# Third chunk's output projection in front of the last heads, last gate loaded ahead, last squares summed by TensorE

## The chip, the cores and the metric

The kernel runs on one core of a Trainium2 chip. The metric is the time of one execution on the device in microseconds (us), of which the median over several runs is taken. One core has a matrix engine (TensorE, PE in the profile), a vector engine (VectorE, DVE), an activation engine (ScalarE, ACT), GpSimd (POOL) and SyncE (SP), which in this kernel only issues DMAs; ScalarE issues some too.

## The reference

A decoder trunk of two layers over 2048 positions of width 1024, all in float32. Layer 0 is a gated short convolution; the change does not touch it. Layer 1 is stick-breaking attention with 8 heads of 64 and a gate, an output projection and a last RMSNorm. Cut to that part:

```python
q, g = split(rmsnorm(x, norm_b) @ w_in_b)
z    = (q @ k.T) * 64 ** -0.5
l1m  = where(mask, log_sigmoid(-z), 0)            # strictly causal
o    = exp(where(mask, z + reverse_cumsum(l1m), -inf)) @ v
x    = x + (o * silu(g)) @ w_out_b                # 512 -> 1024
out  = x * rsqrt(mean(x * x, channels) + 1e-6) * norm_f
```

## The kernel before

Activations are held transposed, channels on the 128 partitions, in four chunks of 512 positions (chunk 3 has the longest attention). A float32 product is made of three matmuls: both factors are split into a high and a low part (`split`, L174 to L176: a cast on ScalarE, a subtraction on VectorE or GpSimd), and high times high, high times low and low times high are added in PSUM (`mm3`, L203 to L214; all large projections therefore share line L209).

Attention of one head and chunk (`attention`, L479) goes over chunks of keys. For each, four score tiles `z` (two matmuls each), two sigmoids on ScalarE into `R` and `w`, a running product along the keys on VectorE (`tensor_tensor_scan`, L514), a product (L518), then transposes on TensorE (`wt`, L526), a split of these (L175, L176) and matmuls into `av` (L535, L536). After the last key chunk the two halves of `av` are added into `ot` (L543, L544). GpSimd masks the diagonal and copies the carry (L509 to L513).

After attention of a chunk come these steps:

- `gated(c, k)` (L556) for each pair of heads `k`: the gate `sga` is loaded (L561), the attention output `ogr` too (L566), GpSimd multiplies (L567), and the result is split into `og`. For the last pair of chunk 3, `ot` is still on the core and VectorE multiplies (L563).
- `out_b(c, obs)` (L580): for each of 8 output tiles the weights are loaded, 12 matmuls go into `pob`, the residual `x1o` is loaded and added (L590), the sum is stored to `y_d`, ScalarE squares it and GpSimd adds the square to `acc` (L172).
- `out_stat(c)` (L597): `rstd` sums the squares over channels by four small products with `ones` (L127; the profile counts eight instructions), and takes the inverse root by small VectorE operations (L129 to L141).
- `out_norm(c)` (L601): `bcast` spreads the four columns of `rstd` over a tile (`dg`, L157, two matmuls `prb`, L158); then for 8 tiles a load `x2r` from `y_d` (L607), a scaling on ScalarE (L608), a product on GpSimd (L609) and a store (L610).
- For chunk 3, `out_b_last` (L620) instead: first the products over the first three pairs of heads (9 matmuls a tile into `pob`, added at L630), then the loads of the fourth part of the weights (`whl_obl`, L634); it yields -1.0 there. The rest runs when the last head is done: the gate and split of the last pair, three matmuls a tile into `pol`, an add (L642), a square, sums on VectorE and GpSimd (L649 to L653), `rstd`, and scaling and storing.

The code is written as generators that yield an estimated cost, and `merge` interleaves them: it always advances the stream with the least share of its total done, where the share may be raised to a power (`S7` = 2 for the last heads, which lets them run ahead: the other stream is at half of its total when the heads are at 0.7). The order on each engine is then made by the framework's scheduler from that order and from simulated readiness. Matmuls of the fill are tied to an earlier `av` matmul, the ninth last (`anchors`, `SLACK` = 8), so that they don't run too far ahead. `chain` puts generators in a row, `take` takes a cost's worth, `until` stops at a yielded value, `zipped` alternates. A product of 24 matmuls is one `LIN`; `TO` is 4 of them, one `out_b`.

Two merges matter here (L743 to L751): the `fill` with the first six heads of chunk 3, and the `tail` with the last two. Buffers in rotation: `lin` two PSUM banks, `st` one, `ld` five tiles, weights (`whl`) four, `t` four.

Of the kernel before, what the change touches and what calls it, by code (L numbers as in the profile page):

```python
# [8 lines left out]
F32 = mybir.dt.float32  # L9
# [5 lines left out]
P = 128  # L15
# [30 lines left out]
def kernel(  # L46
# [66 lines left out]
    def st(nm):  # L113
        return psum.tile([P, CH], F32, name=nm, tag="st", bufs=1)
# [2 lines left out]

        return sb.tile([P, 2, CH], F32R, name=f"{nm}_{k}", tag="act", bufs=NA)

    def rstd(acc, nm, y=None):  # L120


        acc = acc if isinstance(acc, (list, tuple)) else [acc]
        ps = st(f"pst_{nm}")
        for j in range(4):
            for i, a in enumerate(acc):
                nc.tensor.matmul(ps[:, j:j + 1], a[:, j * P:(j + 1) * P], ones[:, 0:1], start=i == 0, stop=i == len(acc) - 1)  # L127
        v = sb.tile([P, 4], F32, name=f"v_{nm}", tag="sv")
        nc.vector.tensor_scalar(out=v, in0=ps[:, 0:4], scalar1=1.0 / D, scalar2=EPS, op0=ALU.mult, op1=ALU.add)  # L129

# [30 lines left out]
    def rstd_bcast(acc, nm, both=False):  # L161
        return bcast(rstd(acc, nm), nm, both)
# [390 lines left out]

    og_t = {}

    def gated(c, k, r=None):  # L556

        og = act_tile(f"og_{c}", k)
        og_t.setdefault(c, []).append(og)
        sg = ld512(f"sga_{c}_{k}")  # L560
        nc.sync.dma_start(out=sg, in_=sg_d[c][k])  # L561
        if r is not None:
            nc.vector.tensor_mul(r, r, sg)  # L563
        else:
            r = ld512(f"ogr_{c}_{k}")
            nc.sync.dma_start(out=r, in_=og_d[c][k])  # L566
            nc.gpsimd.tensor_mul(r, r, sg)  # L567
        split(og[:, 0, :], og[:, 1, :], r)
# [51 lines left out]
    def out_b_last(c):  # L620
# [11 lines left out]
        wl = [w_tile(f"obl{i}", 4) for i in range(2)]  # L632
        for ob in range(KD):
            nc.sync.dma_start(out=wl[ob // 4][:, :, ob % 4, :].bitcast(F32), in_=split_d["ob", ob][:, :, 3, :])  # L634
        yield -1.0
        anchors.clear()
        gated(c, 3, last_ot[0])
        acc = [sb.tile([P, CH], F32, name=f"acc_x2{c}_{i}", tag="acc", bufs=2) for i in range(2)]
        for ob in range(KD):
            ps = lin(f"pol_{ob}")  # L640
            yield from mm3(ps, wl[ob // 4][:, :, ob % 4:ob % 4 + 1, :], og[3:4], kt=1)
            nc.vector.tensor_add(x2[ob], x2[ob], ps)  # L642
            if ob < 2:
                nc.scalar.activation(acc[ob], x2[ob], AF.Square)
            else:
                sq = t512(f"sq_x2{c}{ob}")
                nc.scalar.activation(sq, x2[ob], AF.Square)
                if ob in (2, 4):
                    nc.gpsimd.tensor_add(acc[0], acc[0], sq)  # L649
                else:  # L650
                    nc.vector.tensor_add(acc[1], acc[1], sq)
                if ob == 6:
                    nc.vector.tensor_add(acc[1], acc[1], acc[0])  # L653
        pb = rstd_bcast(acc[1], f"x2{c}", both=True)
        pbs = t512(f"pbs_{c}")
        nc.scalar.copy(pbs, pb)
        for k in range(KD):
# [60 lines left out]
    def heads(lo, hi, c):  # L718
        for hb in range(lo, hi):
# [5 lines left out]
            else:  # L725
# [53 lines left out]
```

## Time and profile before

| | us |
|---|---|
| median of three runs | 1880.44 (1878.28 to 1884.79) |
| the profiled execution | 1879.31 |
| its span, first to last instruction | 1877.6 |
| TensorE busy | 1771.9 (94%) |
| VectorE busy | 1261.9 (67%) |
| ScalarE busy | 772.7 (41%) |
| GpSimd busy | 450.4 (24%) |
| mean granted TensorE clock | 0.979 |

Durations and moments come from the profiled execution; its time is 1.7 us above its span. Busy time of TensorE counts overlapping matmuls once; the mean length of one matmul is longer than the distance between two starts. A line number is one of the kernel before; where a line is a helper's, the names of the tiles tell who called it.

### The profile page before, as it was taken

Reading aid. Unit: us, or ns where it says so; the run is one execution under the profiler, and the core shown is the slowest. Engines: PE = TensorE matmul, PEld = TensorE weight load, DVE = VectorE, ACT = ScalarE, POOL = GpSimd, SP = SyncE. Lnnn points to the kernel's source line nnn. Section 1 sums busy time; section 2 is a strip of 40 time slices with the busy share of each in tenths; the row PEclk is TensorE's granted clock in tenths of the full one; section 3 lists DMA queues with packets and bytes.
Section 4 is the critical chain, followed back from the end, with each engine's and each line's share of the span. In section 5 each row is a group of like instructions: output and inputs, shape, how many; then the busy total and the mean of one; then the engine's idle time right before and its main releaser. Section 6 shows DMA issues by size and latency. Waiting matters only on the chain.

```text
span 1877.6 us, 24951 instructions
## 1 busy us (share of the span) xinstructions
PE 1771.9 (94%) x8312; PEld 1447.6 (77%) x8312; DVE 1261.9 (67%) x1927; ACT 772.7 (41%) x1497; POOL 450.4 (24%) x822
## 2 busy tenths in 40 slices
PE   7999999999999999999999999999988998988783
PEld 5888888888778878887888888888766886866562
DVE  7876534554243364478785478787858889889984
ACT  6423212231232143345443244454535556556642
POOL 5100000101111032132221122232223214547543
PEclk9999999999999999999999999999999999999896
DMA  9999865697978798867677766566586667778763
GB/s 292 309 324 332 307 195 165 209 328 280 336 250 281 227 330 257 290 207 250 216 253 244 248 195 204 183 215 198 180 300 196 223 194 265 260 238 278 225 196 130
DMA packets 238480, 460.44 MB, mean 245 GB/s; under 512 B 18448, under 2 KB 133136, under 8 KB 213776
## 3 DMA queue, kind: packets, MB, share of 16 engines
q1 hardware_dynamic: 178272, 400.09, 63.0%
q10 hardware_dynamic: 59920, 58.74, 10.9%
q8 instruction: 66, 1.08, 0.2%
q14 instruction: 62, 0.51, 0.1%
q0 software_dynamic: 160, 0.02, 0.1%
HBM read 322.73 MB, written 136.05 MB: 244 GB/s over the span
## 4 chain that ended last, share of the span: by engine, by line
PE 74%; DVE 10%; DMA 7%; issue 4%; ACT 2%; POOL 2%; SPq 0%; ACTq 0%; POOLq 0%; DVEq 0%
PE pX L209 9%; PE pB L209 9%; PE po L209 9%; PE pG L209 9%; PE pC L209 8%; PE wt L526 4%; PE pv L209 4%; PE pk L209 3%; PE pq L209 3%; DVE R L514 3%; PE pg L209 3%; PE av L536 3%; PE av L535 2%; PE z L500 2%; PE z L501 2%
## 5 line engine op out<-in xcount | busy, mean ns | idle before, releaser
L514 DVE TENSOR_TENSOR_SCAN R<-R,R,ones 128x512 f32<-128x512 f32 x192 | 255.0, 1330 | 25.2 <-ACT R L503 24.7
L503 ACT ACTIVATE R<-z 128x512 f32<-128x512 f32 (+1 forms) x320 | 174.0, 544 | 185.0 <-PE z L501 72.7
L176 DVE TENSOR_TENSOR wtl<-wt,wth 128x512 fp32r<-128x512 f32 (+1 forms) x320 | 186.2, 601 | 79.9 <-ACT wth L175 76.8
L175 ACT CAST wth<-wt 128x512 fp32r<-128x512 f32 (+1 forms) x320 | 159.6, 528 | 184.7 <-PE wt L526 150.3
L518 DVE TENSOR_TENSOR w<-w,R 128x512 f32<-128x512 f32 (+1 forms) x320 | 207.7, 658 | 19.6 <-POOL R L511 2.1
L209 PE MATMUL pC<-h,whl_C 128*128 128x512 f32 x768 | 189.8, 396 | 11.0 <-ACT whl_C L175 8.0
L513 POOL COPY R<-R 128x1 f32<-128x1 f32 x192 | 117.4, 613 | 340.9 <-DVE R L514 308.6
L209 PE MATMUL po<-y,whl_o 128*128 128x512 f32 x768 | 189.2, 393 | 2.4 <-DVE x L394 2.0
L209 PE MATMUL pX<-h,whl_X 128*128 128x512 f32 x768 | 186.3, 392 | 1.3 <-DVE cv L354 1.3
L209 PE MATMUL pB<-h,whl_B 128*128 128x512 f32 x768 | 185.9, 392 | 0.0
L209 PE MATMUL pG<-h,whl_G 128*128 128x512 f32 x768 | 185.7, 392 | 0.0
L526 PE MATMUL wt<-ident,w 128*128 128x128 f32 x1088 | 176.8, 278 | 7.5 <-DVE w L518 4.5
L209 PEld LDWEIGHTS pC<-h,whl_C 128*128 128x128 f32 x768 | 143.5, 189 | 44.1 <-ACT whl_C L175 8.0
L505 ACT ACTIVATE w<-z 128x512 f32<-128x512 f32 (+1 forms) x320 | 172.1, 543 | 2.5 <-PE wt L526 2.4
L209 PEld LDWEIGHTS pX<-h,whl_X 128*128 128x128 f32 x768 | 143.5, 188 | 31.5 <-DVE cv L354 1.5
L209 PEld LDWEIGHTS po<-y,whl_o 128*128 128x128 f32 x768 | 142.7, 188 | 32.1 <-DVE x L394 2.2
L209 PEld LDWEIGHTS pB<-h,whl_B 128*128 128x128 f32 x768 | 143.5, 188 | 29.7
L209 PEld LDWEIGHTS pG<-h,whl_G 128*128 128x128 f32 x768 | 143.6, 188 | 29.5
L526 PEld LDWEIGHTS wt<-ident,w 128*128 128x128 f32 x1088 | 137.4, 143 | 36.0 <-DVE w L518 6.9
L536 PE MATMUL av<-wtl,vv 128*128 128x512 f32 (+1 forms) x320 | 127.3, 401 | 27.0 <-DVE wtl L176 26.5
L514 DVE TENSOR_TENSOR_SCAN R<-R,ones 128x512 f32<-128x512 f32 (+3 forms) x128 | 116.4, 915 | 37.0 <-POOL R L509 32.8
L500 PE MATMUL z<-kt,q 128*128 128x512 f32 (+1 forms) x320 | 129.3, 406 | 5.7 <-ACT w L505 2.8
(172 smaller groups left out, 2685.1 us busy)
## 6 DMA issues: line engine op xcount, KB each, us to landing
whl_o<-sw_o SPq DMA_DIRECT2D x24, 1024.0 KB, 5.3
kt<-k_d ACTq DMA_DIRECT2D x80, 256.0 KB, 4.0
vv<-v_d ACTq DMA_DIRECT2D x80, 256.0 KB, 3.7
whl_C<-sw_C SPq DMA_DIRECT2D x16, 1024.0 KB, 5.9
whl_X<-sw_X SPq DMA_DIRECT2D x16, 1024.0 KB, 5.3
whl_B<-sw_B SPq DMA_DIRECT2D x16, 1024.0 KB, 5.8
whl_G<-sw_G SPq DMA_DIRECT2D x16, 1024.0 KB, 5.3
whl_k<-sw_kv SPq DMA_DIRECT2D x16, 1024.0 KB, 7.0
```

The lines of the kernel that those rows point to most:

```text
L175: nc.scalar.copy(hi, src)
L176: eng.tensor_sub(lo, src, hi.bitcast(F32))
L209: ins = nc.tensor.matmul(ps, w[:, k, :], a[k][:, m, :], start=n == 0, stop=n == 3 * kt - 1)
L500: nc.tensor.matmul(ps[:, lom:CH], q2[:, 0, qi * P:(qi + 1) * P], kt[:, lom:CH], start=True, stop=False)
L501: nc.tensor.matmul(ps[:, lom:CH], q2[:, 1, qi * P:(qi + 1) * P], kt[:, lom:CH], start=False, stop=True)
L503: nc.scalar.activation(R[:, lo + 1:CH + 1], ps[:, lo:CH], AF.Sigmoid, scale=-0.125)
L505: nc.scalar.activation(w[:, lo:CH], ps[:, lo:CH], AF.Sigmoid, scale=0.125)
L513: nc.gpsimd.tensor_copy(R[:, 0:1], carry[qi])
L514: nc.vector.tensor_tensor_scan(out=R[:, lo + 1:CH + 1], data0=R[:, lo + 1:CH + 1], data1=ones[:, 0:1].to_broadcast([P, CH - lo]), initial= ...
L518: nc.vector.tensor_mul(w[:, lo:CH], w[:, lo:CH], R[:, lo:CH])
L526: nc.tensor.transpose(wt[:, qi * P:(qi + 1) * P], ws[qi][:, kb * P:(kb + 1) * P], ident)
L536: ins = nc.tensor.matmul(av[:, 0:n], vs, wl[:, 0:n], start=False, stop=final)
```

## The change

`out_b(2)`, `out_norm(1)` between its parts, and `out_stat(2)` go from the tail into the fill, and the fill's total grows by one `TO`. The tail keeps the gates of the first three pairs of chunk 3, two tiles of `out_b_last` (before: three), `out_norm(2)` and the rest of `out_b_last`. The gate of the last pair is loaded after the last weight loads, in front of what the last heads still issue then. In the last part each square is summed over channels by four small products right behind its tile, added up in one PSUM bank over the eight tiles, in place of sums of tiles on VectorE and GpSimd and one group of products at the end.

```diff
-    def rstd(acc, nm, y=None):
+    def rstd(acc, nm, y=None, ps=None):
-        acc = acc if isinstance(acc, (list, tuple)) else [acc]
-        ps = st(f"pst_{nm}")
-        for j in range(4):
-            for i, a in enumerate(acc):
-                nc.tensor.matmul(ps[:, j:j + 1], a[:, j * P:(j + 1) * P], ones[:, 0:1], start=i == 0, stop=i == len(acc) - 1)
+        if ps is None:
+            ps = st(f"pst_{nm}")
+            for j in range(4):
+                nc.tensor.matmul(ps[:, j:j + 1], acc[:, j * P:(j + 1) * P], ones[:, 0:1], start=True, stop=True)
...
+    def load_sg(c, k):
+        sg = ld512(f"sga_{c}_{k}")
+        nc.sync.dma_start(out=sg, in_=sg_d[c][k])
+        return sg
-    def gated(c, k, r=None):
+    def gated(c, k, r=None, sg=None):
...
-        sg = ld512(f"sga_{c}_{k}")
-        nc.sync.dma_start(out=sg, in_=sg_d[c][k])
+        if sg is None:
+            sg = load_sg(c, k)
...
+        sg = load_sg(c, 3)
         yield -1.0
         anchors.clear()
-        gated(c, 3, last_ot[0])
-        acc = [sb.tile([P, CH], F32, name=f"acc_x2{c}_{i}", tag="acc", bufs=2) for i in range(2)]
+        gated(c, 3, last_ot[0], sg)
+        ps2 = st(f"pst_x2{c}")
         for ob in range(KD):
             ps = lin(f"pol_{ob}")
             yield from mm3(ps, wl[ob // 4][:, :, ob % 4:ob % 4 + 1, :], og[3:4], kt=1)
             nc.vector.tensor_add(x2[ob], x2[ob], ps)
-            if ob < 2:
-                nc.scalar.activation(acc[ob], x2[ob], AF.Square)
-            else:
-                sq = t512(f"sq_x2{c}{ob}")
-                nc.scalar.activation(sq, x2[ob], AF.Square)
-                if ob in (2, 4):
-                    nc.gpsimd.tensor_add(acc[0], acc[0], sq)
-                else:
-                    nc.vector.tensor_add(acc[1], acc[1], sq)
-                if ob == 6:
-                    nc.vector.tensor_add(acc[1], acc[1], acc[0])
-        pb = rstd_bcast(acc[1], f"x2{c}", both=True)
+            sq = t512(f"sq_x2{c}{ob}")
+            nc.scalar.activation(sq, x2[ob], AF.Square)
+            for j in range(4):
+                nc.tensor.matmul(ps2[:, j:j + 1], sq[:, j * P:(j + 1) * P], ones[:, 0:1], start=ob == j == 0,
+                                 stop=ob == KD - 1, skip_group_check=True)
+        pb = bcast(rstd(None, f"x2{c}", ps=ps2), f"x2{c}", True)
...
-                 out_b(1, lo), out_norm(0), out_b(1, hi), gated_in(2), out_stat(1))
-    merge((fill, TR + 2 * TG + 2 * TO), (heads(0, 3, 3), 0.75 * ta(3)))
-    tail = chain(out_b(2, lo), out_norm(1), out_b(2, hi), out_stat(2),
-                 gated_in(3, range(3)), take(last, NB * 9 * MM), out_norm(2), until(last, -1.0))
-    merge((tail, TO + 72 * MM), (heads(3, 4, 3), 0.25 * ta(3), S7))
+                 out_b(1, lo), out_norm(0), out_b(1, hi), gated_in(2), out_stat(1),
+                 out_b(2, lo), out_norm(1), out_b(2, hi), out_stat(2))
+    merge((fill, TR + 2 * TG + 3 * TO), (heads(0, 3, 3), 0.75 * ta(3)))
+    tail = chain(gated_in(3, range(3)), take(last, 2 * 9 * MM), out_norm(2), until(last, -1.0))
+    merge((tail, 72 * MM), (heads(3, 4, 3), 0.25 * ta(3), S7))
```

More of the change, by code (lines that the diff above doesn't have):

```diff
@@ L634, in out_b_last @@
             nc.sync.dma_start(out=wl[ob // 4][:, :, ob % 4, :].bitcast(F32), in_=split_d["ob", ob][:, :, 3, :])
+        sg = load_sg(c, 3)
         yield -1.0
         anchors.clear()
-        gated(c, 3, last_ot[0])
-        acc = [sb.tile([P, CH], F32, name=f"acc_x2{c}_{i}", tag="acc", bufs=2) for i in range(2)]
+        gated(c, 3, last_ot[0], sg)
+        ps2 = st(f"pst_x2{c}")
+        sqs = []
         for ob in range(KD):
```

## The prediction

> **What bounds the kernel now.** I read the page's totals, then the timeline of VectorE for the moments at which attention heads end, then the windows between those moments, and last the timelines of each engine from 1816 us on.
>
> The ends of heads (the add into `ot`, L544); columns are start us, us, engine, line:
>
> ```profile
> span 1877.6 us, 24951 instructions
> ...
> 1731.43 0.69 DVE L544 TENSOR_TENSOR ot<-ot,av 64x512 f32<-64x512 f32 x1
> ...
> 1842.76 0.69 DVE L544 TENSOR_TENSOR ot<-ot,av 64x512 f32<-64x512 f32 x1 [5.65 <-ACT ot L543]
> ```
>
> Six heads of chunk 3 end by 1731.4, the last two by 1842.8. The windows cut there, and at the last scan, the last matmul of attention, the first `pol` and the first step of the final rstd (window, length, then busy us of each engine):
>
> ```profile
> core 0: us, PE busy (x) PEld busy (x) DVE busy (x) ACT busy (x) POOL busy (x), PEclk, DMA share, GB/s
> ...
> 1414.00:1731.40 317.40, 292.82 (x1424) 234.26 (x1423) 281.70 (x373) 185.75 (x372) 134.13 (x206) 0.97 0.72 235
> 1731.40:1817.80 86.40, 68.44 (x312) 52.30 (x312) 83.91 (x122) 53.16 (x103) 47.03 (x58) 0.90 0.72 227
> 1817.80:1837.30 19.50, 19.43 (x93) 15.44 (x91) 12.08 (x30) 4.14 (x7) 6.29 (x5) 0.99 0.62 175
> 1837.30:1847.90 10.60, 0.01 (x1) 0.00 (x0) 2.02 (x3) 3.36 (x5) 3.78 (x3) 0.72 0.71 237
> 1847.90:1862.50 14.60, 10.66 (x32) 7.10 (x32) 9.42 (x14) 7.18 (x11) 2.57 (x2) 0.73 0.02 8
> 1862.50:1877.60 15.10, 1.23 (x2) 0.57 (x2) 6.46 (x23) 1.86 (x5) 3.71 (x3) 0.50 0.40 139
> ```
>
> So the end has five stages with different limits. A, six heads with the fill: TensorE busy 292.8 of 317.4, nearly the bound, 24.6 idle, VectorE 35.7 idle. B, the last two heads up to their last scan: VectorE 83.9 of 86.4. C: TensorE without a gap, though nothing is left to scan. D: nobody works, 10.6 us. E: the last partial projection and its squares. What follows 1862.5 is not touched.
>
> **The moved projection, stage A.** `out_b(2)` brings 8 x 12 matmuls, `out_stat(2)` eight small products, `out_norm(1)` a broadcast. The rates, from the timeline of TensorE:
>
> ```profile
> 1804.01 0.95 PE L127 MATMUL pst_x<-ones,acc_x 128*128 128x1 f32 x8
> ...
> 1819.88 4.38 PE L209 MATMUL pob<-og,whl_ob 128*128 128x512 f32 x18
> 1824.10 0.39 PE L536 MATMUL av<-wtl,vv 128*128 128x512 f32 x1
> ```
>
> 18 matmuls hold the stream for 4.22 us (1819.88 to 1824.10), 0.234 each; 96 make 22.5, with 0.95 and two broadcast products 24 us. Stage A has 24.6 us of TensorE idle, and the waits say of what:
>
> ```profile
> PE av L536 <- DVE wtl L176: 15.3, 16, 2.6
> ```
>
> 15.3 of it is TensorE waiting for VectorE. With more fill between the same heads VectorE is asked for less per microsecond, so some of this closes; but the late part of A has both engines near full, and new waits appear when VectorE gets the new adds. The bounds are 0 (all idle used) and +30 (none used, and 6 lost to new waits). I take a quarter used, **+18**. The same weights, x1 loads, y stores and gates go through SP's queue, now beside those of the gates; the queue has to carry nothing more in all.
>
> What leaves stage B, by its groups (count, busy us, mean ns):
>
> ```profile
> L514 DVE TENSOR_TENSOR_SCAN R<-R,R,ones 128x512 f32<-128x512 f32 x21 | 30.1, 1434 | 0.1
> L518 DVE TENSOR_TENSOR w<-w,R 128x512 f32<-128x512 f32 (+3 forms) x24 | 19.5, 813 | 0.6
> ...
> L176 DVE TENSOR_TENSOR og<-ogr,og 128x512 fp32r<-128x512 f32 x7 | 6.0, 860 | 0.2
> ...
> L590 DVE TENSOR_TENSOR x1o<-x1o,pob 128x512 f32<-128x512 f32 x8 | 5.4, 670 | 0.0
> ...
> L134 DVE TENSOR_SCALAR t_x<-v_x 128x4 int32<-128x4 int32 x2 | 1.6, 782 | 0.0
> L136 DVE TENSOR_SCALAR yr_x<-t_x 128x4 int32<-128x4 int32 x2 | 1.4, 699 | 0.0
> ```
> ```profile
> L609 POOL TENSOR_TENSOR x2r<-x2r,pbs 128x512 f32<-128x512 f32 x8 | 13.4, 1684 | 0.6 <-ACT pbs L604 0.6
> L172 POOL TENSOR_TENSOR acc_x<-acc_x,sq_x 128x512 f32<-128x512 f32 x8 | 11.4, 1424 | 5.9 <-ACT sq_x L171 5.9
> L567 POOL TENSOR_TENSOR ogr<-ogr,sga 128x512 f32<-128x512 f32 x6 | 9.5, 1591 | 0.6 <-DMA ogr<-og_d 0.6
> ```
> ```profile
> L514 DVE TENSOR_TENSOR_SCAN R<-R,R,ones x19: 1268/1279/2368, 1739.2 to 1816.6; 128x512 f32<-128x512 f32 x19
> ```
>
> The eight adds go (5.4), four of the seven `og` splits (3.4), the small operations of two rstds (the two rows shown and the short ones beside them, an estimate of 5), and one broadcast is exchanged for another (0). The eight adds of the last projection, now in C, come in: +5.5 at 0.69. GpSimd has 22 tensor operations in B, and VectorE's are stretched beside them: the scan's mean is 1434 against a median of 1279, 21 x 0.155 = 3.3; `w` (0.69 undisturbed, as the split and add rows) 24 x 0.12 = 2.9. Afterwards 11 or so remain (3 gates, 8 of `out_norm(2)`), half the stretch, -3.1. Sum -11.4. VectorE being at 97%, this comes off the stage until latency binds: I take **-10**, between -14 (the same contention gone wholly) and -2 (waits of GpSimd and SP fill the place, since `out_norm(2)` with its 16 DMAs now stands in the middle of these heads, ahead of six of the eight weight loads).
>
> The `og` split, both inputs in SBUF, takes 860 ns in a mean where the add that reads PSUM takes 670. The Trainium skill, SBUF, section Who interferes with whom, says that a VectorE operation with two SBUF inputs waits for a whole GpSimd instruction that reads SBUF. The trace agrees in kind. By that rule the 20-odd GpSimd operations moved into A could hold VectorE by 1.4 to 1.7 each, some 30 us; with the operations moved A would need 333 us of VectorE, an estimate by that page that gives +16 where I took +18.
>
> **Stage C.** TensorE's matmuls in it:
>
> ```profile
> L209 PE MATMUL pob<-og,whl_ob 128*128 128x512 f32 x58 | 14.8, 399 | 0.1
> ```
>
> At 0.234 these 58 take 13.6 of the 19.5 us. They sit there since the merge gave all 168 matmuls of the tail to these two heads with a squared lag, and `gated_in(3)`, behind `out_b(2)`, had its last split only here:
>
> ```profile
> 1815.89 0.68 DVE L176 TENSOR_TENSOR og<-ogr,og 128x512 fp32r<-128x512 f32 x1
> ...
> 1816.56 1.28 DVE L514 TENSOR_TENSOR_SCAN R<-R,R,ones 128x512 f32<-128x512 f32 x1
> ```
>
> Changed, the tail holds 72 matmuls and its gates come first, so they spread over the 18 us of TensorE's idle time in B and the 22.5 freed there. I leave 15 of them (3.5) in C: **-10**, between 0 and -13.6.
>
> **Stage D, and the gate loaded ahead.** ACT, VectorE and SP in turn:
>
> ```profile
> 1836.92 0.39 PE L536 MATMUL av<-wtl,vv 128*128 128x512 f32 x1
> 1847.91 7.99 PE L209 MATMUL pol<-og,whl_obl 128*128 128x512 f32 x21 [10.60 <-ACT og L175]
> ```
> ```profile
> 1841.41 0.72 ACT L608 ACTIVATE x2r<-x2r,g_f 128x512 f32<-128x512 f32 x1 [2.34 <-DMA x2r<-y_d]
> 1842.15 0.58 ACT L543 COPY ot<-av 64x512 f32<-64x512 f32 x1
> ...
> 1847.23 0.62 ACT L175 CAST og<-ot 128x512 fp32r<-128x512 f32 x1 [1.92 <-DVE ot L563]
> ```
> ```profile
> 1845.89 1.31 DVE L563 TENSOR_TENSOR ot<-ot,sga 128x512 f32<-128x512 f32 x1 [2.44 <-DMA sga<-sg_d]
> ```
>
> The copy of `av` could have run at 1837.3; it stood 4.8 us behind `out_norm(2)`'s scalings, which waited for their loads. The gate then cost 2.4. With `out_norm(2)` at half of the heads (18 of 72, squared lag) and the gate ahead of the last anchors, 0.58 + 0.69 + 1.31 + 0.62 and 0.15 of gaps remain: 3.4 us, **-7.2**. Bounds 0 (`out_norm(2)` still drains at the end: the gate's load stands behind it in SP's queue in both kernels) and -8.
>
> **Stage E, squares on TensorE.** No trace shows this order. The change takes out the sums on VectorE and GpSimd and puts eight small products behind each tile. What it replaces:
>
> ```profile
> 1857.68 0.68 DVE L642 TENSOR_TENSOR x<-x,pol 128x512 f32<-128x512 f32 x1
> ...
> 1859.86 0.69 DVE L651 TENSOR_TENSOR acc_x<-acc_x,sq_x 128x512 f32<-128x512 f32 x1
> 1862.52 0.16 DVE L129 TENSOR_SCALAR v_x<-pst_x 128x4 f32<-128x4 f32 x1 [1.96 <-PE pst_x L127]
> ```
> ```profile
> 1858.39 0.63 ACT L647 ACTIVATE sq_x<-x 128x512 f32<-128x512 f32 x1 [0.76 <-DVE x L642]
> ```
> ```profile
> 1856.37 0.96 PE L209 MATMUL pol<-og,whl_obl 128*128 128x512 f32 x3 [0.47 <-DVE x L642]
> 1860.61 1.87 PE L127 MATMUL pst_x<-ones,acc_x 128*128 128x1 f32 x8 [3.28 <-DVE acc_x L651]
> ```
>
> From the last square (1859.0) to its product's end 3.5 us would become one group. But 64 products are 7.6 us at 0.95 and 15 at the low clock's 1.87. The stream: 8 x (0.70 + 0.95) = 13.2, and 2.0 until the first square is there (0.70 + 0.68 + 0.63): 15.2, with a little for the clock 15.6 against 14.6, **+1**. Best case -1.5 (full clock and the head start used), worst +16 (first rival). A product waits on TensorE for ScalarE's square, and the next tile's `pol` queues behind it unless it was put ahead.
>
> **Sum.** Profiled execution 1879.3 (span 1877.6 and 1.7 around it): 1879.3 + 18 - 10 - 10 - 7.2 + 1 = 1871.1; the median of the three times, 1880.4, is 1.1 above it: 1872.2, **1872**. About 0.3% (5.6 us, 1874.8 to 1886.1 is "same") can be told from no change.
>
> **Rivals.**
> First, slower: the small products serialise stage E. If each tile's products stand on TensorE ahead of the next `pol`, a tile costs 0.96 + 0.68 + 0.63 + 1.41 (between 0.95 and 1.87, the granted clock being 0.73) + 0.1 = 3.8, eight 30 us: +16 instead of +1, 1887. It turns the sign above 3.7 us a tile. For it: the order of emission, and two `lin` buffers. Against it: runs of 18 and 21 matmuls where emission has groups of six and three, so the order is already made by readiness. 0.12.
>
> Second, no change: A takes the whole 24, since both engines are near full in its late part, and B gives 6 back: 1872 + 6 + 4 = 1882. For it: moving work removes none. 0.15.
>
> Third, more gain: A uses 14 us of its idle time (+10) and B gives 13.5: 1872 - 8 - 3.5 = 1860. For it the 15.3 us of waits above. 0.17.
>
> Fourth, the clock: B was granted 0.90 and D and E 0.72 and 0.73, where TensorE idled. With 22.5 us less and some 13.6 from C, B holds 59.5 us of matmuls; at 0.73 they take 73, and with the 18 idle us 91, 14 over my B: 1886. Against it: A and C, dense, have 0.97 and 0.99, and B's idle time is in pieces. 0.06. The Trainium skill, TensorE: Matmul & The Clock Gate, part 1, says that the clock is halved after about 3.4 us of idleness; the low rows of D and E agree, and at half clock B's matmuls would need 107 us, an estimate by that page.
>
> **How the numbers follow.** The forecast's own range is 1864 to 1879, chance 0.50, four fifths of it below 1874.8. Faster: 0.40 + 0.17 = 0.57. Same: 0.10 + 0.12 of the second + 0.02 and 0.03 of the first and fourth = 0.27. Slower: 0.10 + 0.03 + 0.03 = 0.16. The range 1858 to 1888 takes in all cases but their ends.
>
> **What would show it.** Right: the sixth head's end about 18 us later than 1731.4; the last two heads' scans over 10 us shorter; few `pob` after the last scan; `pol` 3 to 4 us after the last `av`; `pol` ahead of the previous tile's products. Wrong: an unmoved idle time in A, `pob` still crowding behind the last scan, scalings of `x2r` after the last `av`, or over 20 us from `pol` to `v_x`.

## The result, and the profile after

The change made the kernel slower: 1893.86 us in the median of eight runs (1885.22 to 1900.7) against 1883.67 for eight runs of the kernel before beside them (1878.28 to 1891.19). The ratio is 1.0055, with a 95% interval of 1.0033 to 1.0077. The forecast was 1872.

The profiled execution of the changed kernel took 1885.22, the shortest of its eight (the next is 1893.18), so its trace holds only part of the loss; that of before, 1879.31, lies 4.4 below its median. Lines stand one or more away from those of before: the scan is L513, `mm3` L208, the add into `ot` L543.

Timeline of VectorE, changed kernel, the ends of the sixth and of the last head (start us, us, engine, line):

```profile
span 1883.4 us, 25049 instructions
...
1753.95 0.69 DVE L543 TENSOR_TENSOR ot<-ot,av 64x512 f32<-64x512 f32 x1
...
1851.49 0.69 DVE L543 TENSOR_TENSOR ot<-ot,av 64x512 f32<-64x512 f32 x1 [1.20 <-ACT ot L542]
```

The sixth head ends 22.5 us later than before, the last one 8.7 later. The windows of the changed kernel, cut at the same events as before (columns as in the prediction; the first begins at 1395, ahead of chunk 3's scans):

```profile
1395.00:1754.00 359.00, 323.74 (x1546) 258.26 (x1544) 299.65 (x409) 194.26 (x389) 135.21 (x214) 0.95 0.74 240
1754.00:1841.20 87.20, 70.06 (x306) 51.75 (x306) 80.97 (x112) 49.51 (x97) 48.64 (x59) 0.88 0.66 214
1841.20:1850.80 9.60, 7.39 (x27) 5.45 (x27) 5.11 (x8) 2.34 (x4) 0.00 (x0) 0.66 0.00 0
1850.80:1853.60 2.80, 0.05 (x1) 0.00 (x0) 1.39 (x3) 1.20 (x2) 0.00 (x0) 1.00 0.00 0
1853.60:1868.50 14.90, 14.88 (x88) 12.63 (x88) 6.19 (x9) 7.21 (x11) 0.00 (x0) 0.88 0.01 2
```

The kernel before, with its first window begun at the same 1395:

```profile
1395.00:1731.40 336.40, 306.01 (x1476) 244.37 (x1474) 284.58 (x377) 188.77 (x378) 135.68 (x208) 0.97 0.73 236
```

| stage | before | after | difference | forecast |
|---|---|---|---|---|
| A, from 1395 to the sixth head's end | 336.4 | 359.0 | +22.6 | +18 |
| B, to the last scan's end | 86.4 | 87.2 | +0.8 | -10 |
| C, to the last `av` matmul | 19.5 | 9.6 | -9.9 | -10 |
| D, to the first `pol` | 10.6 | 2.8 | -7.8 | -7.2 |
| E, to `v_x` | 14.6 | 14.9 | +0.3 | +1 |

C and D came as forecast, E too in this one execution. A cost 4.6 more, and B gave nothing. Put A and B together: 422.8 before, of which VectorE was busy 284.58 + 83.91 = 368.5 and idle 54.3; 446.2 after, 299.65 + 80.97 = 380.6 busy and 65.6 idle. VectorE got 12 us more to do there and idled 11 us more. Those are the two questions for the experiments.

The matmuls of `pob` in A and B, first the kernel before, then the changed one (windows of that tile alone: TensorE, its weight loads, VectorE, clock, DMA share, GB/s):

```profile
1395.00:1731.40 336.40, 52.65 (x194) 36.27 (x194) 10.74 (x16) 0.97 0.73 236
1731.40:1817.80 86.40, 30.04 (x109) 20.48 (x108) 5.36 (x8) 0.90 0.72 227
```
```profile
1395.00:1754.00 359.00, 66.79 (x252) 46.92 (x252) 12.74 (x19) 0.95 0.74 240
1754.00:1841.20 87.20, 28.78 (x108) 19.45 (x108) 8.58 (x13) 0.88 0.66 214
```

Of the 96 moved matmuls 58 landed in A (194 to 252). B kept its count (109, 108), since those that had stood in C took the place. The adds behind them in A and B went from 24 to 32, 5.2 us more, and B now holds 16 products of `out_norm` on GpSimd where it held eight:

```profile
L513 DVE TENSOR_TENSOR_SCAN R<-R,R,ones 128x512 f32<-128x512 f32 x20 | 30.1, 1507 | 0.6 <-ACT R L502 0.6
L613 POOL TENSOR_TENSOR x2r<-x2r,pbs 128x512 f32<-128x512 f32 x16 | 25.3, 1603 | 4.8 <-ACT x2r L612 3.2 <-ACT pbs L608 1.4
```

### The profile page after: what moved, and what is told of

Read it like the earlier page. It is cut to its first block, busy times and chain, and to the rows that moved or that the text cites. A ratio compares the mean times of both kernels' runs of the same rounds, so it can differ in the third digit from the quotient of the medians.

```text
span 1883.4 us, 25049 instructions
## 1 busy us (share of the span) xinstructions
PE 1783.8 (95%) x8368; PEld 1455.4 (77%) x8368; DVE 1263.7 (67%) x1922; ACT 770.8 (41%) x1497; POOL 438.6 (23%) x820
## 4 chain that ended last, share of the span: by engine, by line
PE 72%; DVE 11%; DMA 8%; issue 5%; ACT 2%; POOL 1%; SPq 0%; ACTq 0%; POOLq 0%; DVEq 0%
PE po L208 9%; PE pG L208 9%; PE pB L208 8%; PE pX L208 8%; PE pC L208 8%; PE wt L525 4%; PE pv L208 4%; DVE R L513 4%; PE pk L208 4%; PE pq L208 3%; PE pg L208 3%; PE av L535 3%; PE av L534 2%; PE z L499 2%; PE z L500 2%
## 5 line engine op out<-in xcount | busy, mean ns | idle before, releaser
L513 DVE TENSOR_TENSOR_SCAN R<-R,R,ones 128x512 f32<-128x512 f32 x192 | 256.8, 1340 | 22.5 <-ACT R L502 21.9
L502 ACT ACTIVATE R<-z 128x512 f32<-128x512 f32 (+1 forms) x320 | 174.2, 544 | 187.1 <-PE z L500 85.4
L517 DVE TENSOR_TENSOR w<-w,R 128x512 f32<-128x512 f32 (+2 forms) x320 | 210.3, 665 | 29.8 <-POOL w L508 6.7
L208 PE MATMUL pC<-h,whl_C 128*128 128x512 f32 x768 | 190.5, 396 | 10.9 <-ACT whl_C L174 8.1
L512 POOL COPY R<-R 128x1 f32<-128x1 f32 x192 | 111.2, 580 | 361.2 <-DVE R L513 329.5
L208 PE MATMUL po<-y,whl_o 128*128 128x512 f32 x768 | 189.2, 392 | 2.5 <-DVE x L393 1.6
L208 PE MATMUL pX<-h,whl_X 128*128 128x512 f32 x768 | 186.7, 392 | 1.3 <-DVE cv L353 1.3
L208 PE MATMUL pB<-h,whl_B 128*128 128x512 f32 x768 | 185.9, 391 | 0.7 <-DMA whl_B<-sw_B 0.7
L208 PE MATMUL pG<-h,whl_G 128*128 128x512 f32 x768 | 185.7, 391 | 0.0
L208 PEld LDWEIGHTS pC<-h,whl_C 128*128 128x128 f32 x768 | 143.6, 190 | 44.4 <-ACT whl_C L174 8.1
L208 PEld LDWEIGHTS pX<-h,whl_X 128*128 128x128 f32 x768 | 143.7, 188 | 31.7 <-DVE cv L353 1.5
L208 PEld LDWEIGHTS po<-y,whl_o 128*128 128x128 f32 x768 | 142.6, 188 | 32.2 <-DVE x L393 1.8
L208 PEld LDWEIGHTS pB<-h,whl_B 128*128 128x128 f32 x768 | 143.2, 188 | 30.9 <-issue 1.0
L208 PEld LDWEIGHTS pG<-h,whl_G 128*128 128x128 f32 x768 | 143.4, 188 | 29.8
L513 DVE TENSOR_TENSOR_SCAN R<-R,ones 128x512 f32<-128x512 f32 (+3 forms) x128 | 115.5, 907 | 38.1 <-POOL R L508 34.9
```

The lines of the kernel that those rows point to most:

```text
L208: ins = nc.tensor.matmul(ps, w[:, k, :], a[k][:, m, :], start=n == 0, stop=n == 3 * kt - 1)
L502: nc.scalar.activation(R[:, lo + 1:CH + 1], ps[:, lo:CH], AF.Sigmoid, scale=-0.125)
L512: nc.gpsimd.tensor_copy(R[:, 0:1], carry[qi])
L513: nc.vector.tensor_tensor_scan(out=R[:, lo + 1:CH + 1], data0=R[:, lo + 1:CH + 1], data1=ones[:, 0:1].to_broadcast([P, CH - lo]), initial= ...
L517: nc.vector.tensor_mul(w[:, lo:CH], w[:, lo:CH], R[:, lo:CH])
```

## The experiments

Ratios are to the kernel before, run beside each; the medians of before were 1884.59 (e1 to e4), 1882.4 (e5 to e8), 1883.17 (e9 to e12) and 1885.98 (e13 to e15). Stage lengths come from one profiled execution each, which can lie several us from its kernel's median; two of the same kernel (after and e10) differ by 0.8 in A, 2.1 in B and 9.5 in E. All are in this table, with A + B split into VectorE's busy and idle time where the text uses it.

| kernel | A | B | C | D | E | A + B: busy + idle | ratio (95% interval) |
|---|---|---|---|---|---|---|---|
| before | 336.4 | 86.4 | 19.5 | 10.6 | 14.6 | 368.5 + 54.3 | 1 |
| after | 359.0 | 87.2 | 9.6 | 2.8 | 14.9 | 380.6 + 65.6 | 1.0055 (1.0033 to 1.0077) |
| e1 gate alone | 341.6 | 85.4 | 19.5 | 10.5 | 14.6 | 366.3 + 60.7 | 1.0018 (1.0002 to 1.0033) |
| e2 squares alone | 344.4 | 86.2 | 18.9 | 10.1 | 15.3 | 368.2 + 62.3 | 1.0025 (1.0005 to 1.0046) |
| e3 move alone | 360.7 | 86.7 | 10.1 | 2.8 | 14.0 | 381.9 + 65.5 | 1.0029 (1.0013 to 1.0046) |
| e4 after, no products | 360.3 | 77.9 | 7.0 | 2.8 | 15.5 | 368.0 + 70.2 | 0.9961 (0.9941 to 0.9982) |
| e5 after, a third of the matmuls | 356.0 | 91.8 | 8.5 | 2.8 | 15.0 | 382.2 + 65.6 | 1.0035 (1.0013 to 1.0057) |
| e6 before, late `out_norm(2)` | 344.1 | 85.4 | 20.6 | 2.8 | 15.4 | | 0.9984 (0.9968 to 0.9999) |
| e7 e6, tail spread | 343.1 | 91.8 | 12.6 | 2.8 | 14.9 | 375.0 + 59.9 | 0.9982 (0.9968 to 0.9996) |
| e8 after, late `out_norm(2)` | 358.2 | 83.2 | 9.6 | 2.8 | 23.8 | | 1.0056 (1.0035 to 1.0077) |
| e9 after, old squares | 356.2 | 87.9 | 10.0 | 2.8 | 14.0 | | 1.0019 (1.0003 to 1.0036) |
| e10 after, again | 358.2 | 89.3 | 10.2 | 2.8 | 24.4 | | 1.0043 (1.0019 to 1.0067) |
| e11 after, kept warm | 356.9 | 87.7 | 12.2 | 2.8 | 14.4 | | 1.0029 (1.0015 to 1.0044) |
| e12 after, old total | 335.6 | 87.2 | 16.3 | 8.7 | 15.3 | 367.4 + 55.3 | 1.0013 (0.9990 to 1.0035) |
| e13 e9, old total, late `out_norm(2)` | 342.0 | 88.6 | 17.2 | 2.8 | 15.9 | | 0.9961 (0.9941 to 0.9981) |
| e14 e13, no power in the merge | 344.7 | 88.3 | 17.2 | 2.8 | 15.2 | | 0.9959 (0.9942 to 0.9975) |
| e15 before, new total | 360.5 | 84.1 | 15.6 | 10.4 | 14.6 | 372.0 + 72.6 | 1.0030 (1.0015 to 1.0045) |

### The three parts, each alone

**e1**, the gate loaded ahead:

```diff
+        sg = load_sg(c, 3)
         yield -1.0
-        gated(c, 3, last_ot[0])
+        gated(c, 3, last_ot[0], sg)
```

> The kernel before with one part of the change, the gate of the last pair loaded ahead of the last anchors. Theory (the gate waited 2.4 us on its load, everything else of the change costs or is neutral): the add into ot is followed by its product at once, stage D 10.6 us becomes 8.2, total -2. Rival (the load's place in SP's queue, behind the stores of out_norm(2), decides, so that loading earlier in the program does nothing): 0.

D stayed at 10.5. The timelines of ScalarE, SP's queue and VectorE, one line of e1 each:

```profile
1845.84 0.72 ACT L613 ACTIVATE x2r<-x2r,g_f 128x512 f32<-128x512 f32 x1 [2.46 <-DMA x2r<-y_d]
1846.58 0.58 ACT L543 COPY ot<-av 64x512 f32<-64x512 f32 x1
```
```profile
1846.49 0.33 SPq L558 DMA_DIRECT2D sga<-sg_d  x1
```
```profile
1850.63 0.69 DVE L568 TENSOR_TENSOR ot<-ot,sga 128x512 f32<-128x512 f32 x1 [2.75 <-DMA sga<-sg_d]
```

The gate's load was issued at 1846.49, as late as the copy of `av`: it stands behind `out_norm(2)`'s transfers in SP's queue, and the copy behind its scalings on ScalarE. The edit alone saves nothing. Nor is it needed: in e3 below, which does not have it, D is 2.8 as in the whole change.

**e2**, the squares on TensorE, with the code of the change in `out_b_last` and `rstd`:

```diff
+            for j in range(4):
+                nc.tensor.matmul(ps2[:, j:j + 1], sq[:, j * P:(j + 1) * P], ones[:, 0:1], ...)
-        pb = rstd_bcast(acc[1], f"x2{c}", both=True)
+        pb = bcast(rstd(None, f"x2{c}", ps=ps2), f"x2{c}", True)
```

> The kernel before with one part of the change, the last squares summed over channels by TensorE tile by tile. Theory (the small products take the place of the sums one for one): stage E stays at 14.6 us within 1, total 0. Rival (TensorE binds the end, and with the low clock after the long gap of stage D it binds more than in the changed kernel): E 18 us or more, total +4.

E took 15.3 in the profiled execution, and the time is up by 0.25%.

**e3**, the lines of `fill`, `tail` and the two merges alone:

```diff
+                 out_b(2, lo), out_norm(1), out_b(2, hi), out_stat(2))
+    merge((fill, TR + 2 * TG + 3 * TO), (heads(0, 3, 3), 0.75 * ta(3)))
+    tail = chain(gated_in(3, range(3)), take(last, 2 * 9 * MM), out_norm(2), until(last, -1.0))
+    merge((tail, 72 * MM), (heads(3, 4, 3), 0.25 * ta(3), S7))
```

> The kernel before with the move alone: third chunk's projection in the fill, two tiles of the last projection before out_norm(2); gate and squares as before. Theory (the move is the cause: six heads longer by 22, nothing gained up to the last scan, 10 saved behind it and about 5 in stage D): 1.0055 less the gate's 2 us, so +5 to +12 us. Rival (the move is even and the squares cost): 0 to +2.

The stages are those of the whole change: A + B up by 24.6, C and D down by 17.2. The move carries all of these, and is slower by itself: 0.29%, 4.4 us of the median.

### Who pays in A and B

**e4** leaves out `out_norm`'s product with the inverse norm, on GpSimd:

```diff
-            nc.gpsimd.tensor_mul(t, t, pbs)
```

> The changed kernel without GpSimd's product in out_norm: the first three chunks' outputs are stored without their rstd. Theory (the last two heads did not get shorter since 16 of these 24 products now lie beside their scans and stretch VectorE by about 0.5 us each): the stretch from the sixth head's end to the last scan falls from 86.5 us to 78, the total by 6 to 12 us against the changed kernel, so that it stands at 0 or a little below the kernel before. Rival (VectorE's own work binds there whatever GpSimd does): 86 stays, total +8 as with the changed kernel.

```profile
1755.30:1833.20 77.90, 64.76 (x308) 50.27 (x308) 74.70 (x116) 50.01 (x98) 25.41 (x44) 0.96 0.71 236
```

B fell by 9.3 against after, with 16 fewer products in it: 0.58 us of the VectorE-bound stretch for each product on GpSimd (0.71 against the 89.3 of e10). A kept its 360. The median fell by more than the stages of these two traces do, to 1876.43; E of e4 is one of the short ones, and how often it is long in e4 the record doesn't show.

**e5** issues only high times high of `out_b(2)`, so 64 of its 96 matmuls are left out; adds, loads, stores and order stay:

```diff
+                if one and (m or w is lo):
+                    n += 1
+                    continue
...
-            yield from mm3(ps, wts, og, kt=4)
+            yield from mm3(ps, wts, og, kt=4, one=c == 2)
```

> The changed kernel with a third of the moved matmuls: chunk 2's output projection uses the high parts alone (4 of 12 matmuls a tile), everything else stays. Theory (the first six heads with their fill are paid by TensorE, at 0.234 us a matmul: 58 of the 96 run there): that stretch (1395 us to the sixth head's end) falls from 359 us by 9 (39 matmuls), the rest stays since VectorE binds it; total about even with the kernel before, -9 against the changed one. Rival (the stretch grew by VectorE's adds, by GpSimd or by waits for loads): 359 stays, total +8 to +10.

```profile
1395.00:1751.00 356.00, 318.88 (x1504) 253.79 (x1502) 296.42 (x403) 194.53 (x389) 136.57 (x213) 0.94 0.74 244
1751.00:1842.80 91.80, 70.59 (x286) 52.46 (x286) 85.77 (x119) 49.69 (x96) 54.63 (x60) 0.82 0.63 199
```

The two windows hold 62 matmuls fewer than after's (1504 + 286 against 1546 + 306), 14.5 us at the prediction's 0.234. A + B is 447.8, no less than the 446.2 of after, and A is 356.0 where 350 was expected. TensorE's busy time fell by 4.3 only, at a lower granted clock (0.94 and 0.82 for 0.95 and 0.88), so the run took less off TensorE than was meant; but of these 4.3 nothing came off the stretch either. That the moved matmuls' time on TensorE is the price of A, as the prediction had it, finds no support here.

**e6** takes `out_norm(2)` out of the last heads without the move: before with the gate ahead, the broadcast in the old place, and the eight tiles issued behind the last `pol`, their later scalings held behind the last square:

```diff
-                 gated_in(3, range(3)), take(last, NB * 9 * MM), out_norm(2), until(last, -1.0))
+                 gated_in(3, range(3)), take(last, NB * 9 * MM), norm_head(2), until(last, -1.0))
...
+        run(out_norm(2))
         pb = rstd_bcast(acc[1], f"x2{c}", both=True)
```

> The kernel before, the projection of the third chunk not moved; the broadcast of out_norm(2) stays in the tail, but its eight tiles are issued in the last stage, beside the last partial projection, the last four scalings behind the last square on ScalarE; gate loaded ahead. Theory (the 10.6 us without work are the wait for out_norm(2), and nothing else needs them): stage D 3 us, E within 1 us of 14.6, total -7 us. Rival (ScalarE and GpSimd are needed in E, or the stores delay the end): E or the time behind it grows by 4 or more, total -3 to +2.

D fell from 10.6 to 2.8 with no projection moved. Since the gate alone did nothing (e1), the whole of D's gain belongs to `out_norm(2)` being elsewhere. It is worth 0.16% here, 3 us of the 7.8: C, E and what follows E were 1.1, 0.8 and 1.1 longer than before.

**e7** is e6 with the third projection still in the tail, but the gates first and the merge without its power:

```diff
+    tail = chain(gated_in(3, range(3)), out_b(2, lo), out_norm(1), out_b(2, hi), out_stat(2),
+                 take(last, NB * 9 * MM), norm_head(2), until(last, -1.0))
+    merge((tail, TO + 72 * MM), (heads(3, 4, 3), 0.25 * ta(3)))
```

> As the last one, and the tail starts with the gates of the first three pairs of chunk 3 and is merged without the lag (share not squared), so that the matmuls that crowd behind the last scan can run in TensorE's idle time beside the last heads. Theory: C falls from 19.5 to about 9, B grows by the 5 us of the eight adds of VectorE: -12 us in all. Rival (VectorE binds B and TensorE's order makes the heads wait): B grows by 10 or more, total -7 as without it or worse.

```profile
1738.10:1829.90 91.80, 75.92 (x356) 59.17 (x356) 90.74 (x139) 53.54 (x105) 49.95 (x60) 0.94 0.73 238
```

Against e6 C gave 8.0, and B took 6.4, not the 5 that were expected: what came from C into B is paid there nearly in full, VectorE being busy 90.74 of 91.80.

**e8** is the changed kernel with e6's late `out_norm(2)` (e6's edits of `norm_head`, `out_norm` and `run`).

> The changed kernel with the eight tiles of out_norm(2) issued in the last stage instead of beside the last two heads. Theory (each GpSimd product beside the scans costs VectorE 0.55 us, since leaving out 16 of them shortened the stretch by 9): B falls from 87 to 83, total -4 against the changed kernel, +3 to +6 against the kernel before. Rival (only out_norm(1)'s products, which fall on the start of the seventh head, cost): B 87, total +8 to +10.

```profile
1753.20:1836.40 83.20, 66.86 (x302) 50.10 (x301) 77.53 (x110) 46.42 (x91) 43.99 (x56) 0.92 0.66 205
1848.80:1872.60 23.80, 23.57 (x88) 20.64 (x88) 6.15 (x10) 9.53 (x15) 2.90 (x3) 0.53 0.03 12
```

B fell by 4.0 for eight products, 0.5 each, in line with e4 (0.76 each against the B of e10). E, however, took 23.8 at a granted clock of 0.53, and the ratio stayed at 1.0056.

### The last stage and the clock

**e9** is the change without e2's edit: the squares are summed as before.

> The changed kernel with the last squares summed as before, on VectorE and GpSimd. Theory (in the run with out_norm(2) in the last stage the whole stage ran at half the granted clock and took 23.8 us instead of 14.9: the 64 small products make the last stage depend on the clock that TensorE has after the last heads, and the changed kernel's times, 1885 once and 1893 to 1901 seven times, are fast and slow clocks): without them -4 to -6 us against the changed kernel's median, and a narrower spread. Rival (the products cost nothing, the spread comes from the long stretch before): 0.

1.0019, against 1.0055 and, run beside e9 (e10 below), 1.0043 for the whole change: the squares on TensorE cost 0.24 to 0.36%. The intervals overlap, but e2, the direct test, had 0.25. That is the part which the profiled execution of after did not show.

**e10** is the changed kernel once more, unaltered; **e11** the same with 19 matmuls whose result nobody reads, ten tied to one of the last `av` matmuls (`anchors[-5]`) and nine to the last, so that TensorE is not idle ahead of E:

```diff
+        names = [anchors[-5].ins.name, anchors[-1].ins.name]
...
+        for nm, cnt in zip(names, (10, 9)):
+            for i in range(cnt):
+                ins = nc.tensor.matmul(wps, onesr, og[i % 3][:, 0, :], start=True, stop=True)
+                tc.add_manual_dep(ins.ins, nm, PACE, reason="warm")
```

> The changed kernel once more, for the spread of its times and a second look at its last stage. Theory: the last stage is either about 15 us (full clock) or about 24 (half), the times fall in two groups 9 us apart, and a look with a time near 1893 has the long one. Rival: stage E 15 us in every look, the times differ by the stretch before the last scan.

> The changed kernel with 19 more matmuls whose result nobody reads: ten in the gaps behind the last scans, nine behind the last attention matmul, so that TensorE does not idle ahead of the last stage. Theory (the clock decides the last stage): E stays at 14 us or less, the median falls by 4 to 7 us against the changed kernel, less the 1 us by which the nine may delay the first pol. Rival (clock not the cause): 0 to +3.

This time the profiled execution of e10 was a typical one (1896.35, its median 1892.53). Its window of E, then two lines of TensorE's timeline, and the same two of after:

```profile
1855.60:1880.00 24.40, 24.31 (x88) 21.41 (x88) 6.20 (x10) 7.20 (x11) 0.00 (x0) 0.50 0.00 1
```
```profile
1861.43 1.63 PE L208 MATMUL pol<-og,whl_obl 128*128 128x512 f32 x3
1862.85 1.70 PE L653 MATMUL pst_x<-ones,sq_x 128*128 128x1 f32 x8
```
```profile
1858.61 0.94 PE L208 MATMUL pol<-og,whl_obl 128*128 128x512 f32 x3
1859.40 0.95 PE L653 MATMUL pst_x<-ones,sq_x 128*128 128x1 f32 x8
```

The order is the same in both traces, three `pol` matmuls and then the eight products of the tile before. Every group takes nearly twice as long in e10, because the granted clock is 0.50 from start to end of E. So E has two lengths, 15 and 24, by the granted clock. The traces with this stage were the short one in after, e2, e4, e5 and e12 and the long one in e8 and e10. The eight times of the changed kernel, one at 1885.2 and seven from 1893.2 on, leave a gap of nearly that size; those of e10 (1882.8, 1887.0 and six from 1891.8 on) show it less clearly.

The mean clock of E hides what happens in it. Pieces of E (TensorE's busy time, its clock, DMA share, GB/s), for after, e12, e8 and e10 (the last begins 1.8 us ahead of E):

```profile
1853.60:1854.60 1.00, 0.98 (x3) 1.00 0.00 0
1854.60:1858.00 3.40, 3.40 (x10) 0.51 0.00 0
1858.00:1868.50 10.50, 10.50 (x77) 0.99 0.01 2
```
```profile
1842.70:1847.50 4.80, 4.80 (x13) 0.50 0.01 2
1847.50:1858.00 10.50, 10.44 (x77) 0.99 0.01 2
```
```profile
1848.80:1850.40 1.60, 1.59 (x6) 1.00 0.00 0
1850.40:1872.60 22.20, 21.98 (x84) 0.50 0.03 13
```
```profile
1853.80:1880.00 26.20, 24.35 (x88) 0.50 0.00 1
```

After and e8 enter E at the full clock and lose it within 1.6 us; e12 and e10 enter at half of it. After and e12 have it back 4.4 and 4.8 us behind the first `pol`, e8 and e10 never. So the clock at the start of E doesn't decide. What E begins with differs by the squares: in the nine traces with the old squares 21 `pol` matmuls run in an unbroken row (7.5 to 8.5 us), and in all nine the full clock is there from 3.8 to 6.2 us behind the first one on. With the squares on TensorE the row is broken after 6 (e8, e11), 9 or 12 (e4), and then `pol` and small products alternate. Where the clock fell, it came back inside that row or at most 0.4 us behind it, or not at all: the alternating part held the full clock where it had it (10 us in after and e12) and did not bring it back in some 20 us of e8 and e10. That the long row is what brings it back is argued from these traces; no run changes the length of the row alone.

And e11:

```profile
1839.60:1851.80 12.20, 9.97 (x38) 7.79 (x39) 5.15 (x8) 2.35 (x4) 0.00 (x0) 0.72 0.00 0
1851.80:1854.60 2.80, 2.15 (x11) 1.38 (x9) 1.41 (x3) 1.20 (x2) 0.00 (x0) 1.00 0.00 0
1854.60:1869.00 14.40, 14.08 (x88) 12.27 (x88) 6.06 (x9) 6.96 (x11) 0.00 (x0) 0.94 0.01 2
```

E is 14.4 at 0.94, at the full clock for its first 12.8 us, while C is 2.6 us longer than after's. The median is 1888.41 against 1892.53 and the twelve times lie within 7.8 us (1883.1 to 1890.9) where e10's eight lie within 15. The intervals overlap (1.0019 to 1.0067 and 1.0015 to 1.0044), so the size of the gain isn't settled.

### The pace

The merge of `fill` and six heads holds the fill to the same share of its total as the heads of theirs. With `3 * TO` in place of `2 * TO` it issues more fill per head from the start. **e12** keeps all of the change but this number; **e15** makes the opposite edit, alone, in the kernel before:

```diff
-    merge((fill, TR + 2 * TG + 3 * TO), (heads(0, 3, 3), 0.75 * ta(3)))
+    merge((fill, TR + 2 * TG + 2 * TO), (heads(0, 3, 3), 0.75 * ta(3)))
```

> The changed kernel with the fill's declared total left as before, so that the first six heads are issued at the old pace and the moved projection comes behind them, ahead of the seventh head. Theory (the stretch up to the last scan is one stretch bound by VectorE; it grew by 13 us of VectorE's work and by 5 us of idle time, since more fill between the early heads holds them back where TensorE binds): 4 to 5 scans more by 1620 us, and from 1395 us to the last scan 441 instead of 446, total -4 against the changed kernel. Rival (pace does not matter, the work sets the stretch, or the projection at the end of the fill holds up the seventh head): 446 or more, total 0 to +5.

> The kernel before with one number changed: the fill's declared total is larger by one projection, as in the changed kernel, while no work is moved. Pace theory (more fill between the early heads holds them back where TensorE binds, and VectorE, idle then, can't make it up later): 66 or 67 scans by 1620 us instead of 69 to 72, 5 to 8 us more idle time of VectorE up to the last scan, total +4 to +8. Work theory (only the VectorE work that was moved ahead of the last scan counts): the stretch stays at 423 to 430 us, total 0 to +1.

Windows, e12, then e15:

```profile
1395.00:1730.60 335.60, 303.58 (x1474) 243.09 (x1473) 284.18 (x377) 188.11 (x377) 134.75 (x208) 0.97 0.73 235
1730.60:1817.70 87.10, 74.01 (x328) 56.08 (x328) 83.22 (x122) 53.94 (x104) 46.73 (x58) 0.88 0.75 241
```
```profile
1395.00:1755.50 360.50, 321.64 (x1523) 254.85 (x1521) 294.80 (x399) 194.35 (x389) 132.66 (x211) 0.95 0.72 236
1755.50:1839.60 84.10, 70.35 (x309) 53.96 (x309) 77.21 (x107) 49.54 (x97) 41.95 (x54) 0.88 0.63 202
```

e12 has A and B of before to within a microsecond (422.7, where 441 was expected), though its profiled execution was the shortest of its twelve, 10.6 us below the median. The `out_b(2)` that was "moved" then runs behind the sixth head after all (193 `pob` matmuls in A, 132 in B), and C and D come back to 16.3 and 8.7. e15, in which nothing has been moved, has A + B of the change: 444.6, with VectorE's idle time up from 54.3 to 72.6. And it is slower by 0.30% (its interval 0.15 to 0.45). Its profiled execution, 1897.23, was the longest of its runs, so the 21.8 us by which its A + B grew are more than the median's loss of 4.9.

Single executions scatter, but the two totals don't overlap: A lies between 335.6 and 344.7 in the eight traces with the old one (before, e1, e2, e6, e7, e12, e13, e14; mean 341.5) and between 356.0 and 360.7 in the nine with the new one (mean 358.4).

Where the idle time comes from is seen in the scans done early. Windows of the scan alone (VectorE, clock, DMA share, GB/s), for before, after and e15:

```profile
1397.00:1500.00 103.00, 40.02 (x34) 0.98 0.66 213
1500.00:1620.00 120.00, 46.99 (x38) 0.99 0.73 241
```
```profile
1397.00:1500.00 103.00, 36.50 (x31) 0.95 0.65 207
1500.00:1620.00 120.00, 42.93 (x36) 0.96 0.76 253
```
```profile
1397.00:1500.00 103.00, 35.43 (x30) 0.97 0.65 218
1500.00:1620.00 120.00, 40.83 (x34) 0.94 0.72 239
```

Between 1397 and 1620 before did 72 scans, after 66 (one crosses 1500 and stands in both windows), e15 64. With the old total it is 69 to 72 in all eight traces, with the new one 64 to 66 in all nine. For each scan TensorE did 3.7 to 4.0 matmuls of the fill (into `pg`, the projections of the gates, and `pob`) with the old total, 4.4 to 4.8 with the new one. In e15 these are no more in all than in before (284 and 285), beside fewer scans, with a granted clock of 0.95 for 0.98; but e1, at 0.95 too, did 70. The full windows of before show TensorE the busier engine up to 1620, 112.26 against VectorE's 103.17, and VectorE the busier one from there on:

```profile
1500.00:1620.00 120.00, 112.26 (x555) 90.56 (x554) 103.17 (x135) 70.08 (x141) 40.01 (x73) 0.99 0.73 241
1620.00:1720.00 100.00, 86.36 (x401) 67.60 (x400) 91.00 (x125) 57.27 (x115) 63.58 (x74) 0.93 0.77 248
```

My reading, argued from these counts: the greater share of fill there holds back the heads, and these come later, where VectorE is busy 91 of 100 us and can't catch up.

**e13** draws the conclusion: e9 (gate ahead, squares as before, move in program order) with the old total and the late `out_norm(2)` of e6. **e14** is e13 with the power taken from the last merge:

```diff
-    merge((tail, 72 * MM), (heads(3, 4, 3), 0.25 * ta(3), S7))
+    merge((tail, 72 * MM), (heads(3, 4, 3), 0.25 * ta(3)))
```

> The changed kernel with three things taken back or moved: the fill's declared total as before, the last squares on VectorE and GpSimd as before, out_norm(2)'s eight tiles issued in the last stage. Theory: up to the last scan 425, C 16, D 3, E 15 whatever the clock: -8 us against the kernel before, ratio 0.996. Rival (the gap D only moves, to the end or to C): 0.999 or more.

> As e13, with the tail merged without the lag. Theory (fewer matmuls of the last projection behind the last scan, their eight adds ahead of it): C 12, up to the last scan 430, total as e13 within 3 us. Rival (the tail issued earlier takes TensorE and VectorE from the last heads): up to the last scan 437 or more, total 0.999.

```profile
1842.80:1845.50 2.70, 0.00 (x0) 0.00 (x0) 1.38 (x2) 1.20 (x2) 0.00 (x0) 0.89 0.73 194
1845.50:1861.40 15.90, 11.30 (x32) 7.74 (x32) 10.19 (x14) 9.42 (x15) 6.37 (x5) 0.71 0.15 47
```

The two lines are D and E of e13. Both kernels are faster than before by about 0.4% (1877.81 and 1879.19 against 1885.98) and beat the changed kernel; the power of the merge makes no difference between them.

## Why the prediction was wrong

The failed step is the pair of A and B. I priced A by TensorE's idle time and credited B with VectorE's work that leaves it, -10, as if these were separate stages. They are one stretch, from the first scan to the last, and what it needs of VectorE is every add, split and scan that must be done before its end. The sum took 11.4 us of VectorE's time out of B; it fell by 2.9 (83.91 to 80.97), while A's rose by 15.1 (284.58 to 299.65), which the sum for A, made of TensorE's time, put at nothing. Judged by the whole stretch the move removes nothing. It brings in the eight adds of the last projection and eight of `out_norm(2)`'s products, which used to stand behind the last scan: 368.5 us of VectorE became 380.6. Of these 12.1 us the adds are 5.2 and the eight products 4.0 to 4.6 by e8 and e4; the rest I haven't itemised. "The eight adds of the last projection, now in C, come in" stood in B's sum, but the operations that left B were taken as gone when they had only gone to A, and B's adds into `pob` rose from 8 to 13.

A's +18 was +22.6 in this pair of traces and +17 between the means of the two totals: near it, and for the wrong reason. In e5 less of TensorE's time for the moved matmuls shortened nothing; e15 shows that the larger total, with nothing moved, gives the same A (360.5). The diff names that total, and the prediction priced no pace at all: it is the term that was missing. The estimate by the Trainium skill, SBUF, section Who interferes with whom, was +16 for A, from GpSimd's operations moved into it. GpSimd's time in A did not rise at all (135.68 to 135.21), so that wasn't the way either. Nor do the terms printed with it give its 333 us: 281.7 + 30 + 13.8 is 325.5, which would be +8.

B's half-stretch, -3.1, rested on GpSimd being emptier. It was not: 59 operations for 58, because `out_norm(2)` brought eight products more, at 0.5 to 0.58 us of VectorE each (e8, e4).

C (-9.9 for -10) and D (-7.8 for -7.2) were right in size. For D half of the stated condition was right: e6 shows that `out_norm(2)` is the whole cause, and the gate's load ahead does nothing, neither alone (e1) nor in the change (e3 has 2.8 without it).

E, +1, was right where the clock was granted and wrong where it wasn't: +0.3 in after's shortest run, +9.8 in e10. The first rival had the size (+16, "a tile costs 3.8, eight 30 us") for another cause. The order of matmuls was the one that I had argued for, `pol` ahead of the previous tile's products; what decided was the clock, which the forecast counted as "a little" after reading 0.73 for E of before, where TensorE was busy 10.66 of 14.6 us. The prediction puts the turn of the sign at 3.7 us a tile; there the loss would be clear of noise, but by the sum's own terms the sign turns at 3.0 (14.6 + 1 + 8.2 is 23.8 for eight), and E of e10 is 3.05 a tile. The fourth rival looked for the clock in B, which held 0.88.

Put together by the runs: pace alone +0.30% (e15), squares on TensorE +0.24 to +0.36% (e2, e9), and the rest of the change, given this pace, between nothing and a small gain (e9, with the pace and the rest but not the squares, 1.0019 against e15's 1.0030, intervals overlapping): its savings in C and D are mostly paid for in A and B. Together that is about the 0.55% measured. The second rival, no change for want of idle time, was nearest in kind: moving removes no work.

What stays open: A differs by up to 9 us between traces with the same total (335.6 to 344.7 with the old one), so that the split of the 23 us into 12 of work and 11 of idle time is that of one pair of traces; e3 and e5 put it at a similar place. Why one execution gets its clock back in E and another of the same kernel doesn't (after, e10) isn't known, and e12's and e15's median difference to the whole change rests on intervals that touch or overlap.

## What to carry to other kernels

When two streams are interleaved, price a moved piece over the whole stretch that the busiest engine limits, and for every engine: what leaves the end of the stretch for its beginning is not saved, and what had stood behind its end is added. A total handed to a merge is a pace for everything in it; try it alone before crediting or blaming the move. In a short serial tail, look at the granted clock piece by piece before breaking its first row of large products with small ones that an idle engine can do.

## What the runs showed of the hardware

In E of e10 TensorE is busy 24.31 of 24.40 us by the records, with groups of three 512-column matmuls and eight one-column products, and the granted clock stays at 0.50 to the end. The same alternation kept the full clock where it had it: 0.99 over the last 10.5 us of E in after and in e12. The Trainium skill, TensorE: Matmul & The Clock Gate, part 1, has the throttle released by activity, within a few microseconds. The traces agree where E begins with 21 large matmuls in a row: the full clock is there after 3.8 to 6.2 us in all nine. They don't agree in e8 and e10 as far as busy time in the records is activity: some 20 us of it released nothing.

A product of 128x512 on GpSimd, 1.6 us long, costs the VectorE-bound stretch beside it 0.58 us (e4) or 0.5 us (e8), and 0.71 or 0.76 if B of e10 is taken for that of after. The Trainium skill, SBUF, section Who interferes with whom, has the loser wait for the whole instruction; on average over this mix of operations it was a third to a half of one.
